# Splitting q and k on all 128 partitions and stacking the halves by DMA, with a convolution moved behind two score tiles

## The chip, the cores and the metric

The kernel runs on one core of one Trainium2 chip. The metric is the device time of one execution in microseconds (us); a comparison takes the median of several runs. Engines are named as in the profile: PE is TensorE's matmuls and PEld its weight loads, DVE is VectorE, ACT is ScalarE, POOL is GpSimd, SP is SyncE. SP computes nothing: it issues DMAs, in program order, and waits in that order too.

## What is computed

Two layers of a diffusion backbone on 512 latent tokens and 256 context tokens, width 1024. Each layer's mixer has three branches that read one projection `z = h @ w_in`; cut to what the change touches:

```
# branch B: 8 heads, each with two maps a = 0, 1 of 64 columns
q, k = rope(rmsnorm(z_q)), rope(rmsnorm(z_k))          # context: no rope
s[a] = (q[a] @ k[a].T) * 64 ** -0.5
p[a] = softmax(s[a])
attn = (p[0] - lam * p[1]) @ v
# branch C: a short convolution along the tokens, per channel
gb, gc, xin = split(z_c, 3)
y_c  = gb * dwconv3(gc * xin, conv_w)
```

In layer 0 latents ask latents and context (768 keys) and the context asks itself; in layer 1, the last, only the latents ask (512 queries, 768 keys). A gated merge of the branches, an output projection and a feed-forward network with its own convolution follow; the change leaves those alone.

## The kernel before

Activations lie with channels on partitions and tokens along the free axis. Products that need float32 accuracy are made of three passes: each operand is split into a rounded high part (an ACT copy into fp32r) and the rest (a DVE subtraction), and high by high, high by low and low by high are summed in PSUM. `Stream` keeps the weights coming: SP loads a 128x1024 tile (`wraw`, L62), ACT casts it (L83), DVE makes the low part (L69); a load waits until the low part two tiles earlier is made, since two raw tiles are kept.

The order of work is written by hand: generators yield estimated costs, and `weave` (L37) advances the one that is least far along. After each step `tick` calls `Stream.low`, which puts pending low parts on DVE's queue and new loads on SP's. Each engine then works its own queue strictly in order.

In each layer the attention stage (L1300 to L1353) takes 8 heads in turn:

- `project(h + 1)` (q/k and v projection of the next head, its norm and rope) is woven into `attn(h)`.
- `turn(h)` (L1333) follows: `qk_tr` (L711) woven with one half of branch C's projections (`fill(1)`), then `v_tr` (L750).
- `attn(h)` (L888) comes next. Its first step is `scores` for the first tile of 128 queries, so these matmuls stand right behind `v_tr` on PE, with no other PE work between.

`qk_tr` works in three thirds of 256 tokens (c = 0, 1, 2). PE transposes q and k of the third into one PSUM tile (L721), with map a = 0 on partitions 0 to 63 and a = 1 on 64 to 127. For each map ACT writes the high part into `qk` on the map's own 64 partitions (L726), and DVE writes the low part across to the other 64 (L727). So `qk` holds, for each map, high and low stacked on 128 partitions, and one matmul over 128 rows sums two products. A second tile `qw` holds q alone with the halves exchanged, and two DMAs of SP per third fill it from `qk` (L730). In layer 1 the last third is context, k alone, and needs no `qw`. A score tile is `qk` by `qk` plus `qw` by `qk` (L838), for all 768 keys in pieces of 512 and 256, for a = 0 and then a = 1. Two PSUM tiles S hold the two maps; DVE finds the row minimum (L845), ACT takes the exponential and frees S (L847), and DVE combines the maps (L859) a tile later.

Branch C's halves are made by `c_fill` (L777), in a fixed order over four channel blocks i. A half with b = 1 copies its projection into `cp` (ACT), one with b = 2 multiplies it in (DVE), and the one with b = 0 does the convolution (`conv`, L988: one ACT and two DVE instructions for each segment of tokens) after three quarters of its matmuls, and then multiplies the result by the projection in PSUM (L799). Layer 0 has segments of 512 and 256 tokens, layer 1 one of 512. The block i = 0 runs beside the projection of head 0, and the blocks i = 1, 2, 3 have their convolution in the turns of heads 1, 4 and 7. SP writes the result to DRAM (L818) when the next half begins.

Of the kernel before, what the change touches and what calls it, by code (L numbers as in the profile page):

```python
# [11 lines left out]
F32 = mybir.dt.float32  # L12
F32R = mybir.dt.float32r
I32 = mybir.dt.int32
AF = mybir.ActivationFunctionType
ALU = mybir.AluOpType
# [4 lines left out]
NL, NC, T, D = 512, 256, 768, 1024  # L21
# [108 lines left out]
class Net:  # L130
    def __init__(self, tc, d, out):
        self.tc, self.nc, self.d, self.out = tc, tc.nc, d, out
        self.later, self.pre, self.cp, self.defer = [], {}, {}, None
        self.bg = iter(())
        self.np = 0
        self.sq_eng = self.nc.vector

# [490 lines left out]
    def qk_proj(self, l, h, pool, st):  # L628
        nc = self.nc
        wa = self.ws.take("qk", l, h, 0)  # L630
        wb = self.ws.take("qk", l, h, 1)
        zs = pool.tile([128, 2, 6, 128], F32, tag="zs", bufs=1, name="zs")
        ss = pool.tile([128, 3, 8], F32, tag="ss", bufs=1, name="ss")
        def stats(c):
            q0 = 0 if l == 0 or c < 2 else 1
            sq = pool.tile([128, 2, 256], F32, tag="rt", bufs=2, name="sq")
            nc.scalar.activation(sq[:, q0:], zs[:, q0:, 2 * c:2 * c + 2, :].rearrange("p q b c -> p q (b c)"), AF.Square)
            nc.vector.tensor_reduce(ss[:, c, 4 * q0:], sq[:, q0:].rearrange("p q (s c) -> p (q s) c", c=64), AX.X, ALU.add)

        for b in range(6 if l == 0 else 4):  # L640
            ps = self.mm.tile([128, 512], F32, tag="mm", name="mm")
            for k in range(8):
                hi, lo = (wa, wb)[k // 4]
                c = (k % 4) * 256
                hh, hl = self.h[k]
                sl = slice(b * 128, b * 128 + 128)
                nc.tensor.matmul(ps[:, :256], lhsT=hh[:, sl], rhs=hi[:, c:c + 256], start=(k == 0), stop=False)  # L647
                nc.tensor.matmul(ps[:, :256], lhsT=hh[:, sl], rhs=lo[:, c:c + 256], start=False, stop=False)  # L648
                nc.tensor.matmul(ps[:, :256], lhsT=hl[:, sl], rhs=hi[:, c:c + 256], start=False, stop=(k == 7))  # L649
                if k == 3:  # L650
                    yield 1300
            if b == 5:
                self.ws.ahead()
            nc.scalar.copy(zs[:, :, b, :], ps[:, :256].rearrange("p (q c) -> p q c", q=2))
            if b % 2:
                stats(b // 2)
            yield 1300
        if l == 1:
            ps = self.mm.tile([128, 512], F32, tag="mm", name="mm")
            for k in range(8):  # L660
                hi, lo = (wa, wb)[k // 4]
                c = (k % 4) * 256 + 128
                hh, hl = self.h[k]
                nc.tensor.matmul(ps[:, :256], lhsT=hi[:, c:c + 128], rhs=hh[:, 512:768], start=(k == 0), stop=False)
                nc.tensor.matmul(ps[:, :256], lhsT=hi[:, c:c + 128], rhs=hl[:, 512:768], start=False, stop=False)
                nc.tensor.matmul(ps[:, :256], lhsT=lo[:, c:c + 128], rhs=hh[:, 512:768], start=False, stop=(k == 7))
                if k == 3:
                    yield 1300
            self.ws.ahead()
            kc = pool.tile([128, 2, 4, 64], F32, tag="ry", bufs=4, name="kc").rearrange("p q s c -> p (q s c)")[:, :256]  # L670
            nc.scalar.copy(kc, ps[:, :256])

            def kc_tr():
                pt = self.mm.tile([128, 512], F32, tag="mm", name="mmT")
                for b in range(2):
                    nc.tensor.transpose(pt[:, b * 128:(b + 1) * 128], kc[:, b * 128:(b + 1) * 128], self.ident)
                nc.scalar.copy(zs[:, 1, 4:6, :], pt[:, :256].rearrange("p (b c) -> p b c", b=2))
                stats(2)
            st["kc"] = kc_tr
            yield 1300  # L680
        st["zs"], st["ss"] = zs, ss
# [9 lines left out]
    def qk_rope(self, l, c, pool, st):  # L691
        nc = self.nc
        q0 = 0 if l == 0 or c < 2 else 1
        nq = 2 - q0
        zn = st["zs"][:, q0:, 2 * c:2 * c + 2, :].rearrange("p q b (a e) -> p q (b a) e", a=2)
        rr = st["r"][:, 8 * c + 4 * q0:8 * c + 8].rearrange("p (q s) -> p q s", q=nq)
        nc.vector.tensor_tensor(zn, zn, rr.unsqueeze(3).to_broadcast([128, nq, 4, 64]), ALU.mult)  # L697
        yt = pool.tile([128, 2, 4, 64], F32, tag="ry", bufs=4, name="ry")
        y = yt[:, q0:]
        if c < 2:  # L700
            t2 = pool.tile([128, 2, 4, 64], F32, tag="rt", bufs=2, name="rt")
            cg, sg = self.cosg[:, :, 4 * c:4 * c + 4, :], self.sing[:, :, 4 * c:4 * c + 4, :]
            nc.vector.tensor_tensor(t2[:, :, :, 0:32], zn[:, :, :, 32:64], sg[:, :, :, 0:32], ALU.mult)
            nc.vector.tensor_tensor(t2[:, :, :, 32:64], zn[:, :, :, 0:32], sg[:, :, :, 32:64], ALU.mult)
            nc.vector.tensor_tensor(y, zn, cg, ALU.mult)
            nc.vector.tensor_tensor(y, y, t2, ALU.add)
        else:
            nc.vector.tensor_tensor(y, zn, self.gqk[:, q0:].unsqueeze(2).to_broadcast([128, nq, 4, 64]), ALU.mult)
        return yt, q0

    def qk_tr(self, l, h, pool, st):  # L711
        nc = self.nc
        qk = pool.tile([128, 2, 2, T], F32R, tag="qk", bufs=1, name="qk")
        qw = pool.tile([128, 2, T], F32R, tag="qw", bufs=1, name="qw")
        for c in range(3):
            y, q0 = st.pop(("rope", c))
            t = slice(c * 256, c * 256 + 256)
            pt = self.mm.tile([128, 512], F32, tag="mm", name="mmT")
            for q in range(q0, 2):
                for b in range(2):  # L720
                    nc.tensor.transpose(pt[:, (2 * q + b) * 128:(2 * q + b + 1) * 128],  # L721
                                        y[:, q, 2 * b:2 * b + 2, :].rearrange("p a e -> p (a e)"), self.ident)
            pv = pt.rearrange("p (q t) -> p q t", q=2)
            for i, j in ((0, 64), (64, 0)):
                hi = qk[i:i + 64, q0:, i // 64, t]
                nc.scalar.copy(hi, pv[i:i + 64, q0:])  # L726
                nc.vector.tensor_tensor(qk[j:j + 64, q0:, i // 64, t], pv[i:i + 64, q0:], hi.bitcast(F32), ALU.subtract)  # L727
            if q0 == 0:
                for i, j in ((0, 64), (64, 0)):
                    nc.sync.dma_start(qw[i:i + 64, :, t].bitcast(F32), qk[j:j + 64, 0, :, t].bitcast(F32))  # L730
            yield 2200
        st["qk"], st["qw"] = qk, qw

    def v_proj(self, l, h, pool, st):
# [42 lines left out]
    def c_fill(self, l, pool, scr):  # L777
        nc = self.nc
        segs = self.segs
# [17 lines left out]
        def mul(dst):  # L797
            def f(o, m, ps):
                nc.vector.tensor_tensor(dst[:, o:o + m], dst[:, o:o + m], ps[:, :m], ALU.mult)  # L799
            return f  # L800
# [7 lines left out]
        for i in range(4):  # L808
            if i > 1:
                yield first(i)  # L810
            if i:
                yield half(2, i, mul(ps[i]))
            c = pool().tile([128, T], F32, tag="cc", bufs=1, name="cc")

            def conv(seg):
                self.conv(c, ps[i], [pc[:, PC_CW + 4 * j + i:PC_CW + 4 * j + i + 1] for j in range(3)], None, [seg])
            yield half(0, i, mul(c), mid=conv)
            nc.sync.dma_start(scr[i][:, :n], c[:, :n])  # L818
        self.vg = []
        for i in range(N_VS):  # L820
            v = self.slots.tile([128, T], F32, tag=("B0", "B7")[i], name="vg")
# [3 lines left out]
    def scores(self, pool, st, t0, k0, nk):  # L825
# [5 lines left out]
        for a in range(2):  # L831
            if a == 0 or nk > 512:
                s = self.sp.tile([128, 1024], F32, tag="S", name="S")
            c0 = a * nk if nk <= 512 else 0
            for v in range(2):
                for o in range(0, nk, 512):
                    m = min(512, nk - o)
                    nc.tensor.matmul(s[:, c0 + o:c0 + o + m], lhsT=(st["qw"][:, a] if v else st["qk"][:, 0, a])[:, t0:t0 + 128],  # L838
                                     rhs=st["qk"][:, 1, a, k0 + o:k0 + o + m], start=(v == 0), stop=(v == 1))
            ss.append(s[:, c0:c0 + nk])  # L840
        if nk <= 256:
            nc.vector.tensor_reduce(mn, s[:, :2 * nk].rearrange("p (a k) -> p a k", a=2), AX.X, ALU.min)
# [45 lines left out]
    def attn(self, l, h, pool, st):  # L888
# [9 lines left out]
        for i in range(n + 4):  # L898
# [11 lines left out]
                sc[i] = self.scores(pool, st, *seq[i])  # L910
            if 0 <= i - 1 < n:
                am[i - 1] = self.combine(*sc.pop(i - 1))
            yield left

    @staticmethod
# [628 lines left out]
```

## Time and profile before

| | us |
|---|---|
| median of 3 runs | 2686.05 (2684.03 to 2686.64) |
| profiled execution, its own time | 2683.64 |
| its span in the trace | 2681.9 |
| PE busy | 2611.5 (97%) |
| DVE busy | 1660.8 (62%) |
| ACT busy | 1011.5 (38%) |
| attention stage, layer 0 | about 78 to 540 of the span |
| attention stage, layer 1 | about 1600 to 1998 |

The span is the time from the first to the last instruction in the trace; 1.7 us of the execution lie around it. A busy PE is not a PE at its peak, since matmuls overlap and their ends are modelled; a wait shows as idle time in front of an instruction, with what ended it. DMA issues stand in SP's timeline with the time that SP spent on the issue; the time to landing is counted from the start of the issue.

### The profile page before, as it was taken

How to read it: one execution, taken by the hardware profiler on the slowest of the kernel's cores; microseconds unless marked ns; L12 is line 12 of the kernel's file. 1: busy time of each engine (PE TensorE's matmuls, PEld its weight loads, DVE VectorE, ACT ScalarE, POOL GpSimd, SP SyncE). 2: the span in 40 equal slices, each digit the busy share in tenths (PEclk: the TensorE clock that was granted, in tenths of full speed). 3: DMA queues.
4: the chain of work that ended last, by engine and by line, in shares of the span. 5: the costliest groups of instructions: out<-in, count | busy, mean ns of one | idle time of the engine just before them, and what ended most of it. 6: DMA issues, size and time to landing. Idle time of an engine off the chain costs nothing.

```text
span 2681.9 us, 36899 instructions
## 1 busy us (share of the span) xinstructions
PE 2611.5 (97%) x14952; PEld 2254.3 (84%) x14952; DVE 1660.8 (62%) x2895; ACT 1011.5 (38%) x1711; POOL 220.6 (8%) x202
## 2 busy tenths in 40 slices
PE   8999999999999999999999999999999999999999
PEld 3889989888888888888888878888878888888887
DVE  5677877756556437544544567877867554654444
ACT  3455455442122224312322334554553232342432
POOL 0000000001111110100100100000001122020101
PEclk8999999999999999999999999999999999999999
DMA  5211221224233331222222232212125545233333
GB/s 224 81 44 58 57 69 48 58 73 146 96 126 105 108 134 63 79 79 79 79 79 79 85 104 67 67 51 65 56 69 171 175 164 180 71 95 102 94 103 110
DMA packets 79658, 254.33 MB, mean 95 GB/s; under 512 B 9200, under 2 KB 19712, under 8 KB 79104
## 3 DMA queue, kind: packets, MB, share of 16 engines
q1 hardware_dynamic: 64512, 196.64, 22.8%
q0 software_dynamic: 14544, 55.07, 6.4%
q8 instruction: 118, 1.93, 0.3%
q14 instruction: 52, 0.43, 0.0%
q10 hardware_dynamic: 432, 0.27, 0.0%
HBM read 234.63 MB, written 6.82 MB: 90 GB/s over the span
## 4 chain that ended last, share of the span: by engine, by line
PE 78%; DVE 14%; ACT 5%; issue 2%; DMA 1%; DVEq 0%; POOL 0%; SPq 0%; ACTq 0%; POOLq 0%
PE mm L183 22%; PE mm L186 21%; PE mm L184 21%; DVE wlo L69 3%; PE S L838 2%; ACT pa L847 2%; PE mm L647 2%; PE mm L648 2%; PE mm L649 2%; DVE qk L727 2%; ACT whi L83 1%; PE mmT L871 1%; DVE mn L845 1%; ACT qk L726 1%; DVE zs L697 1%
## 5 line engine op out<-in xcount | busy, mean ns | idle before, releaser
L183 PE MATMUL mm<-hh,whi 128*128 128x512 f32 (+1 forms) x2392 | 854.5, 357 | 11.9 <-ACT hh L376 9.8
L184 PE MATMUL mm<-hl,whi 128*128 128x512 f32 (+1 forms) x2392 | 819.1, 353 | 4.4 <-DVE hl L379 4.1
L186 PE MATMUL mm<-hh,wlo 128*128 128x512 f32 (+1 forms) x2392 | 752.2, 353 | 1.3 <-DVE wlo L69 1.3
L183 PEld LDWEIGHTS mm<-hh,whi 128*128 128x128 f32 x2392 | 452.2, 189 | 104.7 <-ACT hh L376 13.3
L184 PEld LDWEIGHTS mm<-hl,whi 128*128 128x128 f32 x2392 | 452.4, 189 | 69.0 <-DVE hl L379 9.3
L69 DVE TENSOR_TENSOR wlo<-wraw,whi 128x1024 fp32r<-128x1024 f32 x320 | 399.4, 1249 | 179.2 <-ACT whi L83 177.5
L186 PEld LDWEIGHTS mm<-hh,wlo 128*128 128x128 f32 x2392 | 414.3, 190 | 41.5 <-DVE wlo L69 3.5
L83 ACT CAST whi<-wraw 128x1024 fp32r<-128x1024 f32 x320 | 334.6, 1047 | 291.7 <-PE mm L184 250.1
L996 DVE SCALAR_TENSOR_TENSOR cv<-mm,pc,cv 128x511 f32<-128x511 f32 (+1 forms) x132 | 86.8, 658 | 181.8 <-ACT cv L995 180.9
L183 PE MATMUL mm<-ah,whi 128*128 128x512 f32 (+1 forms) x528 | 187.9, 356 | 0.0
L847 ACT ACTIVATE pa<-S,mn 128x768 f32<-128x768 f32 (+1 forms) x160 | 129.3, 813 | 150.1 <-DVE mn L845 122.6
L647 PE MATMUL mm<-whi,hh 128*128 128x256 f32 x640 | 183.3, 286 | 1.3 <-DVE cp L775 0.8
L648 PE MATMUL mm<-wlo,hh 128*128 128x256 f32 x640 | 181.1, 283 | 0.8 <-DVE wlo L69 0.8
L649 PE MATMUL mm<-whi,hl 128*128 128x256 f32 x640 | 180.9, 283 | 0.0
L184 PE MATMUL mm<-al,whi 128*128 128x512 f32 (+1 forms) x528 | 179.9, 354 | 0.0
L186 PE MATMUL mm<-ah,wlo 128*128 128x512 f32 (+1 forms) x528 | 161.7, 355 | 0.0
L995 ACT ACTIVATE cv<-mm,pc 128x512 f32<-128x512 f32 (+1 forms) x132 | 88.7, 705 | 177.2 <-PE mm L186 177.2
L1157 DVE SCALAR_TENSOR_TENSOR x<-mm,mod,x 128x512 f32<-128x512 f32 (+1 forms) x91 | 58.2, 659 | 138.7 <-PE mm L186 138.7
L1200 POOL TENSOR_TENSOR cv<-cv 128x768 f32<-128x768 f32 (+1 forms) x44 | 91.5, 2080 | 605.2 <-DVE cv L998 420.7
L647 PEld LDWEIGHTS mm<-whi,hh 128*128 128x128 f32 x640 | 121.7, 190 | 4.2 <-ACT cp L773 1.0
L648 PEld LDWEIGHTS mm<-wlo,hh 128*128 128x128 f32 x640 | 122.0, 191 | 1.3 <-DVE wlo L69 1.2
L649 PEld LDWEIGHTS mm<-whi,hl 128*128 128x128 f32 x640 | 121.9, 190 | 0.0
(232 smaller groups left out, 4028.4 us busy)
## 6 DMA issues: line engine op xcount, KB each, us to landing
wraw<-w SPq DMA_DIRECT2D x320, 512.0 KB, 3.6
araw<-ada POOLq DMA_DIRECT2D x80, 512.0 KB, 4.0
qw<-qk SPq DMA_DIRECT2D x80, 128.0 KB, 2.5
araw<-ada SPq DMA_DIRECT2D x16, 512.0 KB, 7.4
x<-xT SPq DMA_DIRECT2D x8, 384.0 KB, 6.1
srow<-sscr POOLq DMA_DIRECT2D x3, 1024.0 KB, 5.4
x<-xT POOLq DMA_DIRECT2D x8, 384.0 KB, 5.9
xscr<-x SPq DMA_DIRECT2D x8, 256.0 KB, 3.9
```

The lines of the kernel that those rows point to most:

```text
L69: self.lo_eng.tensor_tensor(lo, raw, hi.bitcast(F32), ALU.subtract)
L83: self.nc.scalar.copy(hi, raw)
L183: nc.tensor.matmul(ps[:, :m], lhsT=hh, rhs=xh[:, o:o + m], start=st, stop=False)
L184: nc.tensor.matmul(ps[:, :m], lhsT=hh, rhs=xl[:, o:o + m], start=False, stop=False)
L186: nc.tensor.matmul(ps[:, :m], lhsT=hl, rhs=xh[:, o:o + m], start=False, stop=sp)
L647: nc.tensor.matmul(ps[:, :256], lhsT=hh[:, sl], rhs=hi[:, c:c + 256], start=(k == 0), stop=False)
L648: nc.tensor.matmul(ps[:, :256], lhsT=hh[:, sl], rhs=lo[:, c:c + 256], start=False, stop=False)
L649: nc.tensor.matmul(ps[:, :256], lhsT=hl[:, sl], rhs=hi[:, c:c + 256], start=False, stop=(k == 7))
L847: nc.scalar.activation(pa[:, :nk], ss[a], AF.Exp, bias=mn[:, a:a + 1], scale=-1.0, accum_out=sm[a])
L995: nc.scalar.activation(dst[:, o:o + m], s, AF.Identity, scale=w[1], bias=bias)
L996: nc.vector.scalar_tensor_tensor(dst[:, o + 1:o + m], s[:, :m - 1], w[0], dst[:, o + 1:o + m], ALU.mult, ALU.add)
L1200: nc.gpsimd.tensor_tensor(cs[1][:, :n], cs[1][:, :n], cs[0][:, :n], ALU.mult)
```

## The change

`qk_tr` now makes one ACT copy and one DVE subtraction per third, on all 128 partitions, into a staging tile `hl` (two buffers) that holds high and low parts, both maps, q and k. Nothing is written across partitions by DVE any more. `qk` and `qw` become one tile for each map, with high on partitions 0 to 63 and low on 64 to 127, and all of both is filled from `hl` by DMAs of SP: for each map two for `qk` (q and k, high and low) and two for `qw` (q alone). That is 8 DMAs per third in place of 2 (4 in the context third of layer 1, in place of none). The estimate that `qk_tr` yields falls from 2200 to 1300, so `weave` puts the later thirds earlier in the turn. `ry` has three buffers in place of four.

Branch C's half with b = 0 now copies its projection to a tile `g` (ACT); the convolution is kept as a generator, and `attn` takes one segment of it after its second and its third score tile (i = 1 and 2), followed by the multiplication with `g` in SBUF and the DMA to DRAM. For the last block (i = 3) it is done at once, at the end of the half.

```diff
     def qk_tr(self, l, h, pool, st):
-        qk = pool.tile([128, 2, 2, T], F32R, tag="qk", bufs=1, name="qk")
-        qw = pool.tile([128, 2, T], F32R, tag="qw", bufs=1, name="qw")
+        qk = [pool.tile([128, 2, T], F32R, tag=f"qk{a}", bufs=1, name="qk") for a in range(2)]
+        qw = [pool.tile([128, T], F32R, tag=f"qw{a}", bufs=1, name="qw") for a in range(2)]
...
             pv = pt.rearrange("p (q t) -> p q t", q=2)
-            for i, j in ((0, 64), (64, 0)):
-                hi = qk[i:i + 64, q0:, i // 64, t]
-                nc.scalar.copy(hi, pv[i:i + 64, q0:])
-                nc.vector.tensor_tensor(qk[j:j + 64, q0:, i // 64, t], pv[i:i + 64, q0:], hi.bitcast(F32), ALU.subtract)
-            if q0 == 0:
-                for i, j in ((0, 64), (64, 0)):
-                    nc.sync.dma_start(qw[i:i + 64, :, t].bitcast(F32), qk[j:j + 64, 0, :, t].bitcast(F32))
-            yield 2200
+            hl = pool.tile([128, 2, 2, 256], F32R, tag="hl", bufs=2, name="hl")
+            nc.scalar.copy(hl[:, 0, q0:], pv[:, q0:])
+            nc.vector.tensor_tensor(hl[:, 1, q0:], pv[:, q0:], hl[:, 0, q0:].bitcast(F32), ALU.subtract)
+            hf = hl.bitcast(F32)
+            for a in range(2):
+                r = slice(64 * a, 64 * a + 64)
+                for v in range(2):
+                    nc.sync.dma_start(qk[a][64 * v:64 * v + 64, q0:, t].bitcast(F32), hf[r, v, q0:])
+                if q0 == 0:
+                    for v in range(2):
+                        nc.sync.dma_start(qw[a][64 * v:64 * v + 64, t].bitcast(F32), hf[r, 1 - v, 0])
+            yield 1300
...
     def c_fill(self, l, pool, scr):
...
-            c = pool().tile([128, T], F32, tag="cc", bufs=1, name="cc")
-
-            def conv(seg):
+            g = self.slots.tile([128, T], F32, tag="A6" if i < 3 else "A7", name="cg")
+
+            def conv(c, seg, g=g, i=i):
+                o, m, _ = seg
                 self.conv(c, ps[i], [pc[:, PC_CW + 4 * j + i:PC_CW + 4 * j + i + 1] for j in range(3)], None, [seg])
-            yield half(0, i, mul(c), mid=conv)
-            nc.sync.dma_start(scr[i][:, :n], c[:, :n])
+                nc.vector.tensor_tensor(c[:, o:o + m], c[:, o:o + m], g[:, o:o + m], ALU.mult)
+                if seg is segs[-1]:
+                    nc.sync.dma_start(scr[i][:, :n], c[:, :n])
+
+            def convs(conv=conv):
+                c = pool().tile([128, T], F32, tag="cc", bufs=1, name="cc")
+                for seg in segs:
+                    yield conv(c, seg)
+
+            def gate(i=i, g=g, convs=convs):
+                yield from half(0, i, lambda o, m, q: nc.scalar.copy(g[:, o:o + m], q[:, :m]))
+                self.convs = convs()
+                if i == 3:
+                    for _ in self.convs:
+                        pass
+            yield gate()
...
     def attn(self, l, h, pool, st):
...
             if 0 <= i - 1 < n:
                 am[i - 1] = self.combine(*sc.pop(i - 1))
+            if i in (1, 2):
+                next(self.convs, None)
             yield left
```

`scores` reads `qk[a]` and `qw[a]` in place of `qk` and `qw`, with the same matmuls.

## Rows read from the trace of the kernel before

**Rows 1.** The page: busy time and share of the span of each engine.
```profile
PE 2611.5 (97%) x14952; PEld 2254.3 (84%) x14952; DVE 1660.8 (62%) x2895; ACT 1011.5 (38%) x1711; POOL 220.6 (8%) x202
```
**Rows 2.** Waits, whole span: who waited for whom, us in total, times, longest us.
```profile
ACT qk L726 <- DVE qk L727: 89.0, 48, 4.6
...
PE S L838 <- ACT pa L847: 19.2, 30, 1.2
```
**Rows 3.** Timeline of PE, turn of head 2, layer 0: start, us, line, names, count [idle <-releaser].
```profile
220.17 0.60 PE L721 MATMUL mmT<-ident,ry 128*128 128x128 f32 x4
...
230.46 0.59 PE L838 MATMUL S<-qk 128*128 128x512 f32 x2
...
231.59 0.51 PE L838 MATMUL S<-qk,qw 128*128 128x512 f32 x2
235.85 0.61 PE L838 MATMUL S<-qk 128*128 128x512 f32 x2 [0.88 <-ACT pa L847]
```
**Rows 4.** Timeline of DVE in the same turn.
```profile
223.49 1.22 DVE L69 TENSOR_TENSOR wlo<-wraw,whi 128x1024 fp32r<-128x1024 f32 x1
224.74 0.69 DVE L727 TENSOR_TENSOR qk<-mmT,qk 64x512 fp32r<-64x512 f32 x1
```
**Rows 5.** Timeline of SP's queue in the same turn: the issues.
```profile
224.74 0.33 SPq L62 DMA_DIRECT2D wraw<-w  x1
226.07 1.32 SPq L730 DMA_DIRECT2D qw<-qk  x2
227.43 0.59 SPq L818 DMA_DIRECT2D cscr<-cc  x1
```
**Rows 6.** Lines L730 and L818, whole span: ns of an issue min/median/max; landing.
```profile
L730 SPq DMA_DIRECT2D qw<-qk x80: 590/591/1467, 117.6 to 1965.5; - x80
DMA to landing us min/median/max: 2.3/2.5/5.1
L818 SPq DMA_DIRECT2D cscr<-cc x8: 432/594/608, 119.0 to 1970.7; - x8
```
**Rows 7.** Timelines of PE and SP, turn of head 2, layer 1.
```profile
1730.09 0.60 PE L721 MATMUL mmT<-ident,ry 128*128 128x128 f32 x4
...
1738.87 0.51 PE L838 MATMUL S<-qk,qw 128*128 128x512 f32 x2
...
1732.99 0.33 SPq L62 DMA_DIRECT2D wraw<-w  x1
```
**Rows 8.** Timeline of PE, two turns with a convolution: head 1, layers 0 and 1.
```profile
164.56 0.60 PE L721 MATMUL mmT<-ident,ry 128*128 128x128 f32 x4
...
177.92 0.51 PE L838 MATMUL S<-qk,qw 128*128 128x512 f32 x2
...
1683.19 0.60 PE L721 MATMUL mmT<-ident,ry 128*128 128x128 f32 x4
...
1693.37 0.52 PE L838 MATMUL S<-qk,qw 128*128 128x512 f32 x2
```
**Rows 9.** Tile cc: the convolution's DVE instructions, ns min/median/max.
```profile
L996 DVE SCALAR_TENSOR_TENSOR cc<-cp,pc,cc x12: 475/750/751, 101.3 to 1965.5; 128x511 f32<-128x511 f32 x8, 128x255 f32<-128x255 f32 x4
...
L799 DVE TENSOR_TENSOR cc<-cc,mm x12: 420/683/690, 106.2 to 1968.4; 128x512 f32<-128x512 f32 x8, 128x256 f32<-128x256 f32 x4
```
**Rows 10.** Timelines of ACT, DVE and PE around the third and fourth score tiles, head 2, layer 0.
```profile
244.19 0.90 ACT L847 ACTIVATE pa<-S,mn 128x768 f32<-128x768 f32 x1 [1.62 <-DVE mn L845]
...
248.35 1.82 DVE L845 TENSOR_REDUCE mn<-S 128x1 f32<-128x768 f32 x2 [0.47 <-PE S L838]
...
247.45 0.51 PE L838 MATMUL S<-qk 128*128 128x512 f32 x2
```
**Rows 11.** Stretches: us, busy time (instructions) of each engine, PEclk granted, DMA share, GB/s.
```profile
527.00:531.60 4.60, 1.37 (x14) 1.14 (x11) 3.55 (x8) 2.81 (x10) 0.00 (x0) 1.00 0.36 114
531.70:535.10 3.40, 3.20 (x14) 2.91 (x15) 1.67 (x5) 0.12 (x1) 0.00 (x0) 0.50 0.00 0
1583.00:1589.80 6.80, 5.30 (x13) 3.30 (x12) 6.06 (x10) 3.09 (x5) 0.00 (x0) 0.50 0.25 78
```

More of the change, by code (lines that the diff above doesn't have):

```diff
@@ L133, in __init__ @@
         self.later, self.pre, self.cp, self.defer = [], {}, {}, None
-        self.bg = iter(())
+        self.bg = self.convs = iter(())
         self.np = 0
@@ L669, in qk_proj @@
             self.ws.ahead()
-            kc = pool.tile([128, 2, 4, 64], F32, tag="ry", bufs=4, name="kc").rearrange("p q s c -> p (q s c)")[:, :256]
+            kc = pool.tile([128, 2, 4, 64], F32, tag="ry", bufs=3, name="kc").rearrange("p q s c -> p (q s c)")[:, :256]
             nc.scalar.copy(kc, ps[:, :256])
@@ L697, in qk_rope @@
         nc.vector.tensor_tensor(zn, zn, rr.unsqueeze(3).to_broadcast([128, nq, 4, 64]), ALU.mult)
-        yt = pool.tile([128, 2, 4, 64], F32, tag="ry", bufs=4, name="ry")
+        yt = pool.tile([128, 2, 4, 64], F32, tag="ry", bufs=3, name="ry")
         y = yt[:, q0:]
@@ L712, in qk_tr @@
         nc = self.nc
-        qk = pool.tile([128, 2, 2, T], F32R, tag="qk", bufs=1, name="qk")
-        qw = pool.tile([128, 2, T], F32R, tag="qw", bufs=1, name="qw")
+        qk = [pool.tile([128, 2, T], F32R, tag=f"qk{a}", bufs=1, name="qk") for a in range(2)]
+        qw = [pool.tile([128, T], F32R, tag=f"qw{a}", bufs=1, name="qw") for a in range(2)]
+        both = lambda x: x.rearrange("(v e) q t -> v e q t", v=2)
         for c in range(3):
@@ L837, in scores @@
                     m = min(512, nk - o)
-                    nc.tensor.matmul(s[:, c0 + o:c0 + o + m], lhsT=(st["qw"][:, a] if v else st["qk"][:, 0, a])[:, t0:t0 + 128],
-                                     rhs=st["qk"][:, 1, a, k0 + o:k0 + o + m], start=(v == 0), stop=(v == 1))
+                    nc.tensor.matmul(s[:, c0 + o:c0 + o + m], lhsT=(st["qw"][a] if v else st["qk"][a][:, 0])[:, t0:t0 + 128],
+                                     rhs=st["qk"][a][:, 1, k0 + o:k0 + o + m], start=(v == 0), stop=(v == 1))
             ss.append(s[:, c0:c0 + nk])
```

## The prediction

> **What bounds the kernel now.** The page comes first: PE is busy 97% of the span and the other engines far less [rows 1], so only time in which PE stands still, or runs at a lower clock, can be won or lost. The second view is the waits. The longest entry that this change touches, ACT's copy waiting for DVE's split (89.0 us), is no loss by itself, since ACT isn't the bound; PE's own entries are small. The one to note is the score tile that waits until the exponential has freed S, 19.2 us in 30 times [rows 2].
>
> The third view is a turn in the timelines, engine by engine, because there PE has nothing else to do: the transposes of q and k, half a projection, v's transposes, and then the first score tile, which needs the split of all three thirds. In head 2 of layer 0 the first transposes start at 220.17, the scores at 230.46, and the last score matmul ends at 231.59 + 0.51 = 232.1 [rows 3]: 11.9 us, nearly without idle time. In layer 1 it is 1738.87 + 0.51 - 1730.09 = 9.3 us [rows 7]. Where a convolution stands in the turn it is longer: 177.92 + 0.51 - 164.56 = 13.9 us and 1693.37 + 0.52 - 1683.19 = 10.7 us [rows 8], so 2.0 and 1.4 us are lost there, in three turns of each layer (heads 1, 4, 7).
>
> The fourth view is SP. It issues in order, and its first issue in the turn is a weight load that waits for DVE's low part, 223.49 + 1.22 [rows 4]; it starts at 224.74 and SP is free at about 225.1 [rows 5]. An issue is not free: a `qw` DMA, with two runs per partition, takes 0.59 us of SP. The second of the pair at 226.07 starts 0.59 before the pair's end, at 226.80, and the next issue, which waits for nothing, at 227.43, so the pitch back to back is 0.64 us. A DMA lands 2.3 to 2.5 us after its issue starts [rows 6].
>
> **What the change takes away.** Each third had two copies and two splits of 64 partitions in a chain from ACT to DVE and back; now it has one of each. A split is 0.69 us [rows 4], so DVE is spared 48 of them, some 33 us over 16 turns, and ACT nearly as much. None of it is PE time: it counts only where the scores waited for a split. The same holds of the convolution's two passes and its product, 0.75 + 0.75 + 0.69 = 2.2 us of DVE [rows 9], which leave six turns' first halves (four of them for good; in head 7 they stay at the turn's end). At most the change can win the 3 x 2.0 + 3 x 1.4 = 10 us above, and some 2 us of smaller waits.
>
> **What it adds on the path.** k reached `qk` without a DMA; now both parts of k and q come by DMA, and the first score tile needs the last third. A turn of layer 0 issues 24 DMAs where it had 6, one of layer 1 20 where it had 4, all from one in-order queue that can't start before 225.1, and only then waits for landings. Price of an issue: those of `qk` have two runs per partition, as `qw` had, and I take the 0.64 us pitch. Those of the new `qw`, and of the context third, have one run on 64 partitions, a form that the trace doesn't have. The nearest rows are the weight load (one run, 0.33 + 0.05 = 0.38) [rows 5] and L818 (one run, 0.43 at least, 0.59 behind a `qw`) [rows 6]; I take 0.45. A third then costs 4 x 0.64 + 4 x 0.45 = 4.4 us of SP.
>
> Layer 0: the scores' last need is the low half of k, map 1, third 2. It is the 22nd issue: 225.1 + 2 x 4.4 + 3 x 0.64 + 2 x 0.45 = 236.7. It lands 2.4 later, at 239.1, and the three score matmuls and the pipeline's end behind it take 0.6: 239.7 in place of 232.1, so 7.6 us are lost. Layer 1 begins at 1732.99 + 0.38 = 1733.4 and needs its 20th issue (the last third has four, one run each): 1733.4 + 8.8 + 3 x 0.45 = 1743.5, landed 1745.9, scores over at 1746.5 in place of 1739.4, so 7.1 us. In the six convolution turns 2.0 and 1.4 were lost already, so 5.6 and 5.7 remain. Sum: 5 x 7.6 + 3 x 5.6 + 5 x 7.1 + 3 x 5.7 = 107 us. (Heads 0 differ by their first microseconds and are counted as the others.)
>
> Bounds: at 0.38 us for every issue the turn loses 225.1 + 21 x 0.38 + 2.3 + 0.6 - 232.1 = 3.9 us (layer 1: 4.1). At 0.73, the step within the pair, which also waited for a split, with 3.0 to land, it loses 11.9 (11.5). Summed with the same deductions that is 54 to 177 us. I stay in the middle, since half of the DMAs have the very form of the 0.64 row.
>
> The staging tile has two buffers, so the third third's copy waits until the first third's 8 DMAs have landed: 225.1 + 3.9 + 2.4 = 231.4, split by 232.8, while SP reaches its DMAs at 233.9. That wait is covered by the queue. It does block ACT, and behind it the evacuation of the projection half, the cast of the next weights and, through PSUM, v's transposes; all of these come to about 233, still ahead of the last landing. If the queue were faster this would be the next limit, 1 us away. The weight load behind the turn's DMAs is some 5 us later, and its tile is two casts ahead.
>
> **What is given back.** After a stall PE still does its 2.9 us of projection between the first and second score tile (232.1 to 235.0, then 0.88 idle to 235.85 [rows 3]) while DVE and ACT have nothing left from the turn. The exponential then is early and the 19.2 us of rows 2 go away: -19.
>
> **The clock.** Where PE stood still before, the granted clock fell: busy 1.37 of 4.6 us, then 0.50 (1.2 of 2.4 GHz) for 3.4 us in which PE had work again [rows 11]; it also ran at half for 6.8 us around 1583, in which PE was busy 5.30. A turn after the change is busy some 2 of 9 us at its end, less than the first of these. About 3.4 us at half speed behind each turn lose 1.7 us; with some longer I take 1.8 x 16 = 29. Bounds: 0, and half of 6.8 for each, 54.
>
> **The convolution in `attn`.** Behind score tile 1 DVE gets 2.2 us more, in heads 0, 1 and 4, ahead of the row minimum of tile 2 on its queue, and ACT one pass. The exponential that frees S for tile 3 ends at 244.19 + 0.90 = 245.1, and tile 3 begins at 247.45 [rows 10]: 2.4 us of cover, so nothing. In layer 0 the second segment, two passes of 0.48 and a product of 0.42 [rows 9], stands before a minimum ahead of which DVE idled 0.47. I put 0 for it; with the cover gone the whole would be 3 x 3.6 + 3 x 2.2 = 17 us. Its last DMA goes to a queue that is then waiting for weights.
>
> Sum: 107 - 19 + 29 = 117 us on an execution of 2683.6 (span 2681.9), which lies 2.4 under the median of the runs. From the median, 2686 + 117 = 2803 us.
>
> **A rule weighed.** The Trainium skill, page "DMA: Bandwidth & Descriptors", section "Issuing engines are not separate DMA queues", says that the sequencer's time to start a DMA is usually small against the DMA itself. For one DMA the rows agree in part (0.59 of 2.4 us), for twenty in a row they don't. By that rule the turn would be that of rival 1. The same page, section "Rules for kernel authors", speaks against the change: two transfers to the two halves of the partitions gain nothing over one transfer to all 128.
>
> **Rivals.**
> 1. Faster: the queue keeps up. If the 21 issues before the last needed one fitted between 225.1 and 229.1 (232.1 less 0.6 and 2.4), that is at under 0.19 us each, the scores would never wait and the 10 + 2 us above are won: 2674. Against it: the shortest issue in the rows takes 0.33 us [rows 5]. For it: the form on 64 partitions with one run isn't there. Chance 0.06.
> 2. Cheap issues: all near 0.38, little clock lost: 54 - 19 + 10 = +45, so 2731. For it: the source of a `qk` transfer is one run. Chance 0.13.
> 3. Slow issues and a clock that stays down: 0.73 each and 6.8 us at half. 177 + 54 - 10 = +221, so 2907. For it: issues of up to 1.47 us and landings of 5.1 [rows 6]. Chance 0.09.
> 4. No change that shows, cheap issues and long cover in one: chance 0.03, near 2686.
> The forecast has 0.69.
>
> **How the numbers follow.** The forecast's own range, its issue price between 0.45 and 0.65 throughout and the clock's between 10 and 54, is about 2760 to 2850. Leaving out rivals 1, 3 and 4 and half of 2, the range for 8 in 10 is 2735 to 2865. Faster by over 0.2% (about what a measurement can tell from no change): 0.07; within: 0.03; slower: 0.90.
>
> **What would show it.** In the trace after: SP's queue in a turn without a gap for 11 to 13 us; the score matmuls idle until a DMA of `qk`, 4 to 7 us per turn, 107 us in all; fewer waits of S on the exponential; the clock at 0.50 for 3 us behind turns. I am wrong if SP issues a one-run DMA in 0.2 us or less, or if the scores start beside the queue. A loss spread over score tiles 2 and 3 would speak for the convolution instead.

## The result and the profile after

The kernel before takes 2686.35 us (median of 4 runs, 2684.03 to 2688.31), the changed one 2830.35 us (4 runs, 2829.65 to 2830.96). The ratio is 1.0536, with a 95% interval of 1.0518 to 1.0555: 144 us slower. The forecast was 2803, its range 2735 to 2865.

First the page of the changed kernel, its line of busy times:

```profile
PE 2648.9 (94%) x14952; PEld 2292.0 (81%) x14952; DVE 1629.9 (58%) x2847; ACT 991.9 (35%) x1675; POOL 220.8 (8%) x202
```

Against [rows 1] DVE has 31 us less to do and ACT 20, as the change meant; PE runs the same 14952 matmuls. The span has become 2827.9 us, 146 longer, while PE's busy time rose by 37: most of the loss is idle PE, and the matmuls that were slower are a part of it. The waits of the whole span say on whom PE stands (who waited for whom: us in total, times, longest):

```profile
PE S L858 <- DMA qk<-hl: 116.1, 35, 5.4
...
PE S L858 <- ACT pa L867: 1.7, 3, 0.6
```

And among ACT's waits of the same kernel:

```profile
ACT hl L726 <- DMA qw<-hl: 119.1, 16, 8.4
```

The score matmuls (L858, which answers to L838 of before) now wait for the transfers of `qk`, 35 times; before, DMAs held them for 0.3 us in all. The wait of S on the exponential, 19.2 us in [rows 2], is down to 1.7. ACT's copy into the staging tile waits for a landing once in each of the 16 turns, but ACT isn't what PE waits for, so this line must be followed to its end before it counts.

The turn of head 2 of layer 0, which the prediction worked through, first in PE's timeline (start us, us, engine and line, names, count, idle before it and what ended it):

```profile
236.64 0.60 PE L722 MATMUL mmT<-ident,ry 128*128 128x128 f32 x4
...
249.77 0.44 PE L764 MATMUL mmT<-ident,zv 128*128 128x128 f32 x2 [2.82 <-ACT cp L811]
250.41 0.47 PE L858 MATMUL S<-qk 128*128 128x512 f32 x1 [0.20 <-DMA qk<-hl]
255.77 0.55 PE L858 MATMUL S<-qk 128*128 128x256 f32 x1 [4.89 <-DMA qk<-hl]
...
258.43 0.55 PE L858 MATMUL S<-qk 128*128 128x256 f32 x1 [1.04 <-DMA qk<-hl]
258.78 0.84 PE L858 MATMUL S<-qk,qw 128*128 128x512 f32 x2
```

SP's issues in the same turn:

```profile
241.21 0.33 SPq L62 DMA_DIRECT2D wraw<-w  x1
241.63 1.55 SPq L732 DMA_DIRECT2D qk<-hl  x2
243.24 1.28 SPq L735 DMA_DIRECT2D qw<-hl  x2
...
251.24 1.27 SPq L735 DMA_DIRECT2D qw<-hl  x2
252.60 1.33 SPq L732 DMA_DIRECT2D qk<-hl  x2
253.99 1.26 SPq L735 DMA_DIRECT2D qw<-hl  x2
255.29 1.28 SPq L732 DMA_DIRECT2D qk<-hl  x2
256.61 1.25 SPq L735 DMA_DIRECT2D qw<-hl  x2
257.96 0.53 SPq L62 DMA_DIRECT2D wraw<-w  x1
```

ACT's copies of thirds 2 and 3 into the staging tiles, same turn:

```profile
240.47 0.59 ACT L726 CAST hl<-mmT 128x512 fp32r<-128x512 f32 x1 [2.61 <-PE mmT L722]
248.65 0.59 ACT L726 CAST hl<-mmT 128x512 fp32r<-128x512 f32 x1 [7.59 <-DMA qw<-hl]
```

SP issues 24 transfers from 241.63 to 257.9 with no gap. The score matmul at 255.77 needs `k` of map 0 and third 3, the one at 258.43 that of map 1, the 22nd issue. Turns are compared by one measure here: from the first transposes to the end of the first score tile's matmuls. For this turn it is 258.78 + 0.84 - 236.64 = 23.0 us, where it was 11.9 [rows 3]. In layer 1, head 2, PE's timeline gives 19.3 against 9.3 [rows 7]:

```profile
1823.14 0.60 PE L722 MATMUL mmT<-ident,ry 128*128 128x128 f32 x4
...
1840.00 0.55 PE L858 MATMUL S<-qk 128*128 128x256 f32 x1 [4.20 <-DMA qk<-hl]
...
1841.63 0.84 PE L858 MATMUL S<-qk,qw 128*128 128x512 f32 x2
```

Over the 16 turns, worked out in the same way, the sum was 183 us and is 336: 153 more, while the span grew by 146. So the loss lies in the turns, and everything outside them has become 7 us shorter (the part on why the prediction held divides this up).

### The profile page after: what moved, and what is told of

The parts are those of the page before. It is cut to its first block, busy times and chain, and to the rows that moved or that the text cites. A ratio compares the mean times of both kernels' runs of the same rounds, so it can differ in the third digit from the quotient of the medians.

```text
span 2827.9 us, 37387 instructions
## 1 busy us (share of the span) xinstructions
PE 2648.9 (94%) x14952; PEld 2292.0 (81%) x14952; DVE 1629.9 (58%) x2847; ACT 991.9 (35%) x1675; POOL 220.8 (8%) x202
## 4 chain that ended last, share of the span: by engine, by line
PE 77%; DVE 10%; SPq 6%; ACT 3%; DMA 3%; issue 2%; POOL 0%; DVEq 0%; ACTq 0%; POOLq 0%
PE mm L183 20%; PE mm L186 20%; PE mm L184 20%; PE S L858 3%; SPq L732 3%; SPq L735 3%; PE mm L647 2%; PE mm L648 2%; PE mm L649 2%; DVE wlo L69 1%; DMA qk<-hl 1%; PE mmT L891 1%; DVE al L896 1%; DVE zs L697 1%; DMA wraw<-w 1%
## 5 line engine op out<-in xcount | busy, mean ns | idle before, releaser
L183 PE MATMUL mm<-hh,whi 128*128 128x512 f32 (+1 forms) x2392 | 856.0, 358 | 11.9 <-ACT hh L376 10.0
L183 PEld LDWEIGHTS mm<-hh,whi 128*128 128x128 f32 x2392 | 453.5, 190 | 104.9 <-ACT hh L376 14.3
L858 PE MATMUL S<-qk 128*128 128x512 f32 (+1 forms) x288 | 95.1, 392 | 117.9 <-DMA qk<-hl 116.1
L647 PE MATMUL mm<-whi,hh 128*128 128x256 f32 x640 | 193.1, 302 | 1.3 <-DVE cp L780 0.8
L648 PE MATMUL mm<-wlo,hh 128*128 128x256 f32 x640 | 190.1, 297 | 0.0
L649 PE MATMUL mm<-whi,hl 128*128 128x256 f32 x640 | 189.7, 296 | 0.0
L865 DVE TENSOR_REDUCE mn<-S 128x1 f32<-128x768 f32 x128 | 117.8, 952 | 99.1 <-PE S L858 99.1
L858 PEld LDWEIGHTS S<-qk 128*128 128x128 f32 x288 | 54.2, 212 | 138.2 <-DMA qk<-hl 127.9
```

The lines of the kernel that those rows point to most:

```text
L183: nc.tensor.matmul(ps[:, :m], lhsT=hh, rhs=xh[:, o:o + m], start=st, stop=False)
L858: nc.tensor.matmul(s[:, c0 + o:c0 + o + m], lhsT=(st["qw"][a] if v else st["qk"][a][:, 0])[:, t0:t0 + 128], rhs=st["qk"][a][:, 1, k0 + o:k ...
L865: nc.vector.tensor_reduce(mn[:, a:a + 1], ss[a], AX.X, ALU.min)
```

## Experiments

Each kernel is compared with the kernel before on the same chip. The theory (Q): a turn waits for the issues of SP's queue, and the convolution costs nothing.

**One part at a time.** The first kernel has the new split with the old convolution, the second the old split with the new convolution. The new split includes the lower estimate for `weave` and the three `ry` buffers, which were not run by themselves; in the trace above it is a transfer, and neither of these, that the turn's last score matmuls wait for.

```diff
 # split alone: c_fill as before the change, attn without
-            if i in (1, 2):
-                next(self.convs, None)
 # convolution alone: qk_tr as before the change
```

> The q/k split of the change alone; branch C's convolution stands in the turns of heads 1, 4 and 7 as before. Theory Q (SP's in-order queue): the last DMA that the scores need is still the 22nd (layer 1: the 20th) at 0.66 us each, and DVE has time to spare in the turn, so the convolution there costs nothing more: 2830 us, between 2820 and 2838. Theory C (the loss comes from the convolution between score tiles 2 and 3): near 2690.

> The convolution of the change alone; q and k are split as before. Theory Q: the convolution is covered in attn, and heads 1 and 4 of both layers end their turns 2.0 and 1.4 us earlier, so 2 x 2.0 + 2 x 1.4 = 7 us faster than before: 2679, between 2676 and 2687. Theory C: the larger part of the 144 us, so above 2750.

Split alone: 2833.58 us, ratio 1.0549 (1.0535 to 1.0563). Convolution alone: 2686.37, ratio 1.0004 (0.9995 to 1.0013). The loss belongs to the split. The convolution, though, missed what was expected of it: 2686.37 lies at the slow end of the range, 2676 to 2687, and the 7 us are not there. It does shorten the turns, whose sum is 172 in place of 183 us, so the 10 us were won, and yet the time is unchanged. PE's timeline of this kernel shows where they went, at the fifth score tile of head 0 and the second of head 7 in layer 0:

```profile
141.42 0.38 PE L853 MATMUL S<-qk 128*128 128x256 f32 x1 [1.60 <-ACT pa L862]
...
502.57 0.80 PE L853 MATMUL S<-qk 128*128 128x512 f32 x2 [3.20 <-ACT pa L862]
```

DVE's timeline ahead of the latter says why:

```profile
495.94 0.75 DVE L1013 SCALAR_TENSOR_TENSOR cc<-cp,pc,cc 128x511 f32<-128x511 f32 x1
...
499.15 0.43 DVE L818 TENSOR_TENSOR cc<-cc,cg 128x256 f32<-128x256 f32 x1
...
500.55 1.81 DVE L860 TENSOR_REDUCE mn<-S 128x1 f32<-128x768 f32 x2
```

In layer 0 the first segment was indeed covered, as worked out: it delays the third tile's minimum, and the fourth tile still doesn't wait. But the second segment made the fifth tile late, 1.6 us in heads 0, 1 and 4. In layer 1, which has one segment only, that one was not covered: the fourth tile waited 0.9 us in the same heads. In heads 7 the whole convolution now stands between the turn's last split and the first row minimum: DVE is at it from 495.94 to 499.6, and the second score tile waits 3.2 us (0.66 before). Together that is 4.8 + 2.7 + about 4.7 us (both heads 7, above what they waited before), the whole of the gain.

**Is it the issues?** Half of the turn's transfers go to GpSimd's queue, with nothing else changed:

```diff
-                    nc.sync.dma_start(qk[a][64 * v:64 * v + 64, q0:, t]...
+                    (nc.sync, nc.gpsimd)[a].dma_start(qk[a][64 * v:64 * v + 64, q0:, t]...
 # and the same for qw[a]
```

> The change with the DMAs of map 1 issued by POOL in place of SP, so that each queue has 12 (layer 1: 10) per turn. Theory Q, the price is the issuing queue's time: the last needed one is the 10th or 11th of its queue, 10 x 0.66 = 6.6 us earlier in layer 0 and some 6 in layer 1, if POOL issues at a like price: about 100 us less than the change, 2730, between 2715 and 2760. Theory B, the price is the data's time on the 16 DMA engines, which the queues share: no gain, 2820 to 2835.

2777.2 us, ratio 1.0338 (1.0320 to 1.0357), outside the ranges of both theories; the turns sum to 291 us. So a second queue takes away 53 us of 144, which a limit in the bytes or in the landing alone wouldn't give; but it was to take away 100. The landing shows the rest, in the page's part on DMA issues (KB each, median us from issue to landing), first the changed kernel, then this one:

```profile
qk<-hl SPq DMA_DIRECT2D x160, 128.0 KB, 2.4
...
qk<-hl POOLq DMA_DIRECT2D x80, 128.0 KB, 4.5
qk<-hl SPq DMA_DIRECT2D x80, 128.0 KB, 5.0
```

So does ACT's timeline, at the copy of third 3 in head 2:

```profile
240.71 0.59 ACT L726 CAST hl<-mmT 128x512 fp32r<-128x512 f32 x1 [8.88 <-DMA qw<-hl]
```

A transfer that landed after 2.4 us in the changed kernel now takes 4.5 to 5.0. The first third's transfers therefore free their staging tile only at 240.7, third 3 can't be split before, and its issues start at 241.3. The busy share of the 16 DMA engines in this stretch (the last two numbers of the line are that share and GB/s):

```profile
232.00:247.00 15.00, 7.17 (x46) 6.05 (x45) 4.00 (x6) 3.06 (x6) 6.11 (x11) 0.86 0.82 202
```

The same stretch of the turn in the changed kernel:

```profile
241.60:259.00 17.40, 8.46 (x48) 6.82 (x47) 4.59 (x7) 4.05 (x8) 0.00 (x0) 0.77 0.64 166
```

Whether the bytes are what then limits is tried by two kernels. Both leave the q part of the `qk` transfers out, the first with one queue, the second with two; the number of issues stays, a third of the bytes goes. The scores take `qw` twice instead, so high by high and low by low are left out, and the two mixed products count twice (the expectation of the second kernel names another product); the matmuls are as many.

```diff
-  qk[a][64 * v:64 * v + 64, q0:, t]   <- hf[r, v, q0:]
+  qk[a][64 * v:64 * v + 64, 1:, t]    <- hf[r, v, 1:]
-  lhsT=(st["qw"][a] if v else st["qk"][a][:, 0])[:, t0:t0 + 128]
+  lhsT=st["qw"][a][:, t0:t0 + 128]
```

> The change with k alone in the qk transfers (q's part of that tile is left out, and the scores take qw for both products, so they are not the reference's): as many DMAs, but each carries one run of 1 KB on 64 partitions, half of what the qk ones carried. Theory Q, the price of an issue doesn't hang on its size: within 8 us of the change, 2822 to 2836. Theory B, the price is the data's time: four of eight DMAs per third cost half, some 1.3 us less per third, 3 thirds in 16 turns, about 50 us less than the change: 2780.

> The changed kernel with map 1's transfers issued by GpSimd, and with the q part of the qk transfers left out (the scores take qw for both products, so the high-times-low part of the scores is not computed): the same number of issues as in the run with two queues, a third fewer bytes. Theory E (with two queues the 16 DMA engines are the next limit): 2725 to 2750. Theory P (GpSimd's issue price of about 0.55 to 0.6 us, or the staging tiles, limits the two queues): 2765 to 2778, as with all bytes.

With one queue: 2815.17, ratio 1.0480 (1.0461 to 1.0499). A third fewer bytes gains 15 us: more than the 8 that theory Q allowed, and far less than the 50 of theory B. An issue costs nearly, though not quite, the same whatever it moves: in head 2 of layer 0 the 21 issues ahead of the last needed one take 13.6 us in place of 14.3, and the score matmul starts 2.1 us after the start of that one in place of 2.5. The two together are 1.0 us a turn. The issues of the changed kernel by line, in ns (min/median/max):

```profile
L732 SPq DMA_DIRECT2D qk<-hl x192: 462/616/1552, 112.9 to 2112.1; - x192
...
L735 SPq DMA_DIRECT2D qw<-hl x160: 484/602/679, 114.3 to 2109.6; - x160
```

The same line of this kernel, with one run per partition, 64 KB in all, in place of two runs and 128 KB:

```profile
L732 SPq DMA_DIRECT2D qk<-hl x192: 462/587/1100, 113.3 to 2097.9; - x192
```

With two queues: 2748.96, ratio 1.0230 (1.0216 to 1.0244), at the upper end of what the theory of the DMA engines expected. With two queues the same bytes are worth 28 us and not 15, and the engines' share in the stretch is 0.56. So the transfers do hold the turn once each queue has half of the issues. GpSimd's `qk` issues also became cheaper with the bytes, 0.52 us in place of 0.58 in the mean, so a part of the 28 us may be theirs; the runs don't divide it.

**Fewer issues, and then the staging tile.** The next kernel leaves the swapped operand out, and with it both mixed products of high and low parts (the expectations name one of them), so a turn of layer 0 has 12 issues; the one after has three staging tiles in the memory that this frees.

```diff
-                if q0 == 0:
-                    for v in range(2):
-                        nc.sync.dma_start(qw[a][64 * v:64 * v + 64, t]...
-  lhsT=(st["qw"][a] if v else st["qk"][a][:, 0])[:, t0:t0 + 128]
+  lhsT=st["qk"][a][:, 0][:, t0:t0 + 128]
 # and in the second of the two:
-            hl = pool.tile([128, 2, 2, 256], F32R, tag="hl", bufs=2, name="hl")
+            hl = pool.tile([128, 2, 2, 256], F32R, tag="hl", bufs=3, name="hl")
```

> The changed kernel without the swapped operand: the qw transfers, two sixths of a turn's data but half of the transfers of thirds one and two, are left out, and the scores take qk for both products (so the low-times-high part of the scores is not computed). Twelve transfers of qk remain in a turn of layer 0 and all twelve keep their size. Theory Q (a turn waits for the queue's issues at 0.65 us each): 8 to 10 fewer issues ahead of the last needed one are 5 to 6 us a turn less, but the two staging tiles then give the next limit, third 3's split waiting for third 1's landing near 246.5 instead of 248.6, so 4 to 5 us a turn are won: 2750, 2730 to 2770. Rival S (the staging tiles alone, with the transfers' latency, hold the turn): third 1's landing comes only some 2 us earlier, 2795 to 2815. Rival B (the bytes moved decide): a third fewer bytes, some 2780 to 2790.

> The run without the swapped operand once more (the low-times-high part of the scores is not computed), now with three staging tiles instead of two, in the memory that the swapped operand leaves free; so third 3's split has no transfer to wait for. Theory Q with staging (with a queue of twelve the wait for third 1's landing has become the limit): in the turn of head 2 of layer 0 third 3's first transfer is issued right behind the eighth, at about 234.9 instead of 236.4, 1.5 us a turn: 2728, 2715 to 2738. Rival E (the transfers are held by the 16 DMA engines, which the weight load ahead of them keeps busy until about 234): the last landing doesn't move by more than 0.5 us, 2744 to 2753.

2751.83, ratio 1.0242 (1.0228 to 1.0256), and with three tiles 2731.27, ratio 1.0172 (1.0155 to 1.0189): both within 4 us of theory Q. ACT's copies of thirds 2 and 3 in head 2 of layer 0, with two tiles:

```profile
228.42 0.59 ACT L725 CAST hl<-mmT 128x512 fp32r<-128x512 f32 x1 [2.61 <-PE mmT L721]
235.80 0.58 ACT L725 CAST hl<-mmT 128x512 fp32r<-128x512 f32 x1 [6.79 <-DMA qk<-hl]
```

The twelve issues of that turn in SP's timeline:

```profile
229.55 9.49 SPq L731 DMA_DIRECT2D qk<-hl  x12
```

ACT's two copies with three tiles:

```profile
223.82 0.59 ACT L725 CAST hl<-mmT 128x512 fp32r<-128x512 f32 x1 [2.61 <-PE mmT L721]
225.65 0.59 ACT L725 CAST hl<-mmT 128x512 fp32r<-128x512 f32 x1 [1.24 <-PE mmT L721]
```

And the twelve issues:

```profile
224.97 8.46 SPq L731 DMA_DIRECT2D qk<-hl  x12
```

With two tiles ACT stands 6.8 us for a landing, and the twelve issues take 9.5 us since they pause for it; with three they take 8.5. The turns sum to 261 and 241 us: 20 us less, as the time. So the wait for the staging tile, which is in the list of the changed kernel with 119 us, costs nothing there, because SP reaches third 3 only at 252.60, long after its split at 249.3 to 250.0; it costs 20 us as soon as the queue is shorter. Even the shortest queue, 12 issues, leaves the turns 58 us above those of before. A part of this goes with the landing: on one queue, but with no smaller `qw` transfers between them, the `qk` transfers land after 3.7 us with two tiles and 3.6 with three, at busy shares of the DMA engines of 0.80 (229.5 to 241.5) and 0.85 (225 to 235). The page of the kernel with two tiles:

```profile
qk<-hl SPq DMA_DIRECT2D x160, 128.0 KB, 3.7
```

So a second queue is not needed for a longer landing; it goes with the busy share of the DMA engines.

**The clock.** Fourteen matmuls on data that is there anyway stand ahead of the first score tile's own, in the time in which PE would wait:

```diff
+            if t0 == 0 and a == 0:
+                for _ in range(14):
+                    nc.tensor.matmul(s[:, 0:512], lhsT=self.h[0][0][:, 0:128], rhs=self.h[0][0][:, 0:512], start=True, stop=True)
```

> The changed kernel with 14 matmuls of 512 columns on data that is there anyway, into the first score tile ahead of its first real matmul, so that TensorE works through a part of each stall; the real product begins that bank anew. At full clock they take about 3.1 us, at half clock 6, and in the turn of head 2 of layer 0 they fit between the v transposes at 250 and the score matmul that waits until 255.8. Theory Q with the clock (the half clock during and behind the stall costs 1.2 to 1.8 us a turn): if the clock stays up, 2800 to 2815. Rival N (the clock behind the stall costs nothing, since the waits for DMAs set the pace): 2827 to 2832. If the clock has already fallen when they begin, they stay at half speed and push the next matmuls by up to 1 us a turn: 2832 to 2846.

2818.3 us, ratio 1.0491 (1.0476 to 1.0505): 12 us faster with more work. That lies between the range of theory Q, 2800 to 2815, and that of rival N, 2827 to 2832. The stall and the time behind it in stretches, in the changed kernel (us, busy time of PE, PEld, DVE, ACT and POOL with instructions, granted clock, DMA share, GB/s):

```profile
251.10:261.30 10.20, 4.49 (x16) 3.85 (x17) 3.67 (x5) 2.24 (x5) 0.00 (x0) 0.50 0.63 167
261.40:266.00 4.60, 4.60 (x37) 4.42 (x37) 3.13 (x5) 2.50 (x7) 0.00 (x0) 1.00 0.21 64
```

And with the extra matmuls, whose turn begins 1.9 us earlier in the span:

```profile
248.00:252.00 4.00, 4.00 (x13) 3.24 (x14) 2.29 (x4) 1.88 (x4) 0.00 (x0) 0.61 0.55 135
252.00:256.00 4.00, 2.24 (x10) 1.34 (x8) 0.96 (x1) 0.29 (x1) 0.00 (x0) 1.00 0.66 161
256.00:260.00 4.00, 3.39 (x27) 3.38 (x28) 0.96 (x1) 2.34 (x5) 0.00 (x0) 1.00 0.61 171
```

In the changed kernel PE is granted 0.50 (1.2 of 2.4 GHz) from 251.1 to 261.3, into the work behind the stall. Here the clock is back at full by 252, so the work behind the turn runs at full speed: between the end of the first score tile and the start of the second lie 2.70 us in heads 1 to 5 of layer 0, against 3.5 to 4.9 in the changed kernel. In layer 1 PE still waits for 4 us and more behind the extra matmuls; the clock was at half for 6.8 to 10 us there, and the turns are as long as in the changed kernel. Over all 16 turns this stretch between the first and the second score tile sums to 55.5 us in place of 66.8, while the turns are 1.5 us longer. So the 12 us are won there: they are the price of the clock behind a part of the turns, and the condition of theory Q, a clock that stays up, held behind heads 1 to 5 and 7 of layer 0 alone.

**A version that is faster than both.** The old split, the convolution's two segments behind the fifth and sixth steps of `attn`, where at most one short score tile is still to come, and block 3 as before the change:

```diff
 # qk_tr as before the change; in c_fill block 3 as before the change
-            if i in (1, 2):
+            if i in (4, 5):
                 next(self.convs, None)
```

> The q/k split as before the change. The convolutions of blocks 0 to 2 stand behind the fifth and sixth steps of attention instead of the second and third, where in layer 1 no score tile and in layer 0 only the sixth, short one is still to come; block 3's convolution stays where it was before. Theory Q (the turn ends of heads 1 and 4 fall by 0.9 to 1.9 us as in the run of the convolution alone, and its give-backs, S(4), S(3) and the turns of head 7, don't come): 2679, 2675 to 2684, ratio 0.996 to 0.999. Rival F (VectorE's extra work delays whatever step follows it, here the attention's transposes and their splits): 2686, 2684 to 2690.

2673.55 us, ratio 0.9952 (0.9938 to 0.9965): 12 us faster than before, 1.5 us beyond the range that was expected. PE's entry in the waits:

```profile
PE S L858 <- ACT pa L867: 16.0, 29, 1.2
```

The longest wait of S is 1.2 us, as in [rows 2], and the 19.2 us there are 16.0 here. The turns sum to 173.5 us, 9.5 less than before, with those of heads 7 unchanged; heads 0 gain 2.7 of it, which the expectation had left out. These 9.5 and 3.2 us make up the 12 of the medians. The two profiled executions differ by 8.2 only, since PE of this one was granted 0.50 for 10 us more between the two attention stages (6.8 us at 523.5, 3.4 at 1015 and 3.4 at 1619, against 3.4 at 531.7 before), which cost 4.4 us. Two things differ from the convolution of the change, the later steps and block 3, and no run has one without the other. By the trace of the convolution alone block 3 is the smaller part: its heads 7 lost 4.7 us by the wait and won 3.3 in the turn, while the waits of the fourth and fifth score tiles, which the later steps do away with, were 7.5.

All kernels side by side, the turns worked out as above:

| kernel | 16 turns, us | time, us |
|---|---|---|
| before | 183 | 2686 |
| convolution alone, as in the change | 172 | 2686 |
| convolution later | 173.5 | 2674 |
| 12 issues, three staging tiles | 241 | 2731 |
| 12 issues | 261 | 2752 |
| two queues, a third fewer bytes | 265 | 2749 |
| two queues | 291 | 2777 |
| a third fewer bytes | 324 | 2815 |
| extra matmuls in the stall | 338 | 2818 |
| the change | 336 | 2830 |
| the split alone | 346 | 2834 |

Measured from the change, a microsecond that fewer transfers, fewer bytes or a second queue take out of the turns is 1.0 to 1.2 in the time. The exceptions are the pairs that differ in the place of the convolution, before against the convolution alone and the change against the split alone: there what the turns gain is paid outside them. The extra matmuls act outside the turns too, on the clock behind them.

## Why the prediction held, and where its size was off

**The bound and the mechanism: right.** The cause is SP's in-order queue, as the prediction had it: SP issues without a gap, the scores wait for `qk`'s DMAs, the loss isn't spread over score tiles 2 and 3, and every experiment that shortens the queue shortens the turns.

**The price of a one-run issue: the term that was mis-sized.** The prediction took a pitch of 0.64 us for two runs, and 0.45 for one run on 64 partitions, from the weight load and L818 [rows 5, 6]. The issues of L732 and L735 take 0.616 and 0.602 (medians), both at a pitch of about 0.66: in a burst the form hardly matters. The 0.45 was the price of a one-run issue by itself: the three in the trace with a pause of SP of 0.2 to 0.4 us before them took 0.46 to 0.49, the minima of L732 and L735 above. The 22nd issue starts at 255.95, 19.3 us after the first transposes, where 16.5 was worked out; in layer 1 the end comes at 19.3 where 16.4 was worked out. That is 2.8 us a turn of layer 0, and with the slower matmuls at the turn's end it makes the sum over the turns 153 where 107 stood. The upper bound, 0.73 and 177 us, held it. The 0.59 of L818 behind a `qw` was the nearer row, and it stood in [rows 6]: for a one-run issue what mattered was that it stands behind others.

**The rule weighed.** The Trainium skill, page "DMA: Bandwidth & Descriptors", section "Issuing engines are not separate DMA queues", calls the sequencer's time usually small and a second issuing engine good for that time alone. The first half misleads here: 24 issues at 0.66 us are 16 us of a turn. With the second half the trace agrees: a second queue saved 53 us, and not the 100 that the issues alone would give, since the landing then rose from 2.4 to between 4.5 and 5.0 us.

**The staging tile: right.** It was called covered by the queue and the next limit. Third 3 was copied at 12.0 us into the turn (11.2 worked out) and reached by SP at 16.0 (13.7). With fewer issues it did become the limit, 20 us. It delays v's transposes by 2.8 us, also in the shadow of the queue.

**What is given back: right in kind, larger in size.** The waits on the exponential, 19.2 us of before, are 1.7. The list shows less than they cost, since idle time is counted from the modelled end of the matmul before. At the third score tile of head 2, layer 0, it had 0.25 us; but from the last matmul ahead of the tile to the first one behind it PE took 2.21 us before and takes 1.50 now:

```profile
240.29 0.28 PE L649 MATMUL mm<-whi,hl 128*128 128x256 f32 x1
240.82 0.62 PE L838 MATMUL S<-qk 128*128 128x512 f32 x2 [0.25 <-ACT pa L847]
...
242.50 0.28 PE L647 MATMUL mm<-whi,hh 128*128 128x256 f32 x1
```

```profile
267.31 0.28 PE L649 MATMUL mm<-whi,hl 128*128 128x256 f32 x1
267.43 0.51 PE L858 MATMUL S<-qk 128*128 128x512 f32 x2
...
268.81 0.29 PE L647 MATMUL mm<-whi,hh 128*128 128x256 f32 x1
```

In the kernel with the split alone the stretch from the second score tile to the next turn is 1.0 us shorter in all 14 turns that have another behind them in their layer (36.95 to 35.93 us in layer 0, 32.25 to 31.22 in layer 1).

**The clock: right in kind, smaller in size.** Between the first and the second score tile PE lost 15.8 us of listed waits and yet took 2.7 us longer, summed over the turns: so the slower clock cost 18.5 us there, where 29 was put, or somewhat more, as the waits were longer than listed. At the turns' ends it costs a further few tenths each, which are in the 153. The kernel with the extra matmuls, -12 us, shows that it costs at all.

**The sum, and some luck.** The turns have 153 us more, the stretches between the first and second score tile 2.7 more, the rest of the span 9.9 less: that is the 146 by which the span grew. In the prediction's terms the turns were put 46 us too low, and what lies outside them at +10 (29 less 19) where it came to -7. These two errors go against each other, so the total is off by less than the term that failed. (The forecast's own range, with the ends that it names taken together, works out as 2755 to 2863, wider than the 2760 to 2850 given; the result lies in both.)

**The convolution: wrong, and without weight here.** It was put at nothing, with 17 us as the bound. The cover that was worked out for the first segment was there in layer 0, where it was read, and not in layer 1, for which it was taken over. The other failing steps are the second segment, where a DVE gap of 0.47 us was set against 1.4 us of work, and head 7, whose own order wasn't followed through the row minimum that stands behind the convolution. It gave back all of its 11 us in the kernel with this part alone. In the whole change, the turns' sum is 10 us under that of the split alone but the time only 3: there too most of it is lost again.

## What to carry to other kernels

When a step is traded for DMAs, count the issues on the in-order queue up to the one that the next engine needs, and price them by an issue that stands behind another in a row, not by a lone one. A wait that is covered is covered only by what it was measured against: shorten the queue and the staging tile is the next limit, add a queue and the landing becomes longer. Work moved off a bound engine's path is worth its time only at a place with that much slack on its new queue, step by step; moved three steps later, with block 3 left in its old place, the same convolution kept its gain.

## What the runs showed of the hardware

- A one-run issue of SP costs by its place more than by its size. The same transfer of the convolution's result to DRAM took 0.59 us of SP in the median behind other issues [rows 6], and stood alone in the faster version, where it took 0.33:

```profile
L828 SPq DMA_DIRECT2D cscr<-cc x6: 326/326/330, 151.8 to 1848.2; - x6
```

  Likewise the weight load took 0.33 us ahead of the burst and 0.53 behind it. The two-run `qw` transfers of before took 0.59 at any place: their minimum is 0.590 and their median 0.591 [rows 6], and 33 of the 80 had SP idle for over 0.5 us before them. What SP does in the difference, the trace doesn't show.
- A transfer of 128 KB between two places in SBUF landed after 2.4 us in the changed kernel, at a busy share of the DMA engines of 0.64; after 4.5 to 5.0 with a second queue beside it, at 0.82; and after 3.6 from one queue that held nothing but such transfers, at 0.85.
- A stall of PE was paid for a second time behind it, at half clock, and useless matmuls in the stall bought a part of that back.
